# Final norm of a hybrid decoder step: the last token block in two pieces, and part of the outputs scaled on ScalarE and GpSimd

## The chip, the cores and the metric

The kernel runs on one core of a Trainium2 chip. The metric is the time of one execution on the device, in microseconds (us); lower is better. Times before are three runs, and one more execution was profiled.

## What is computed

The reference is one step of a decoder layer with retention heads, gated DeltaNet heads and a gated MLP, followed by a final norm. The part that matters here is its end, cut to a few lines:

```python
u, buf_ffn_new = causal_depthwise_conv(rms_norm(x, norm_ffn) @ w_up, buf_ffn, conv_ffn)
gate, val = jnp.split(u, 2, axis=-1)
x = x + (jax.nn.silu(gate) * val) @ w_down
...
def rms_norm(x, w):
    y = xf * lax.rsqrt(jnp.mean(xf * xf, axis=-1, keepdims=True) + EPS)
    return y * w
y_prompt = rms_norm(xp[:, N_META:], norm_final)
y_sample = rms_norm(xs, norm_final)
```

There are 1024 features (8 tiles of 128 partitions) and 1058 token columns: 32 sample tokens, 2 columns that are dropped, and 1024 prompt tokens.

## The kernel before

Features lie on the partitions and tokens in the columns. `ob` holds the residual stream, 8 feature tiles m by all columns. The MLP is worked through in 11 groups of two hidden tiles. In each group the up products, a convolution, the gate and the split of the product into a high and a low fp32r part (tiles `al` for the first token block, `as` for the others) come first. Then `down` (L1636) multiplies them with the down weights (`dhl`, `whi`, `wlo`), three matmuls for each of the two hidden tiles, six in all, into one of two PSUM banks of the ring "dn" (`mx3` and `mx4`), and VectorE adds the bank to `ob`, which frees it (L1646).

The token columns are cut by `BLK_B` (L47) into blocks of 510, 274 and 274. In the last group (`tail`), `final` (L1565) is called for each block in turn (L1664). It computes all eight `down` tiles of the block, squares `ob` on ScalarE, and adds the squares into two sums, the even m on GpSimd and the odd m on VectorE (L1576). Then TensorE sums over the partitions with a one-column matmul for each 128 columns (`pss`, L1582). VectorE copies these sums out of PSUM (L1589), scales them, ScalarE takes the root (L1593), VectorE the reciprocal and one step of refinement. A diagonal matrix `dg` for each 128 columns and a matmul with ones (L1603) spread the result over all partitions into the PSUM bank `rb`. VectorE multiplies each of the eight tiles by `nfin(m)` and `rb` in one instruction (L1607), and SP issues its transfer out (L1608).

What sets the order: every operation is recorded (`Recorder`, L209), and `flush` (L367) places all of them by a table of estimated costs and by priority classes, `with cls(n)`, a low number first. Class 0 here is the squares, sums and roots, class 1 the `down` products and additions, class 3 the outputs. So an output runs on VectorE where nothing more urgent is ready by that plan. Every engine then executes its own queue strictly in that order, and all instructions carry line 469 in the profile, where the plan is emitted. Buffers come from rings: "ds" for up to 276 columns, "f2k" for up to 512, and "c3" (names `c` in the profile) for the 128x4 numbers of the roots.

Of the kernel before, what the change touches and what calls it, by code (L numbers as in the profile page):

```python
# [17 lines left out]
AF = mybir.ActivationFunctionType  # L18
ALU = mybir.AluOpType
# [3 lines left out]
P = 128  # L23
D = 1024
# [11 lines left out]
EPS = 1e-6  # L36
# [10 lines left out]
BLK_B = ((0, 510), (510, 784), (784, 1058))  # L47
# [435 lines left out]
def build(tc, I, O, debug=None):  # L483
# [4 lines left out]
    V, S, G, T, DQ = (R.proxy(e) for e in "VSGTD")  # L488
# [11 lines left out]
    def buf(tag, shape, dt=None):  # L500
        v = R.tile(R.rings[tag])
        if dt is not None:
            v = v.bitcast(dt)
        n = 1
        for s in shape[1:]:
            n *= s
        v = v[0:shape[0], 0:n]
        if len(shape) == 3:
            v = v.rearrange("p (a b) -> p a b", a=shape[1])
        elif len(shape) == 4:  # L510
            v = v.rearrange("p (a b c) -> p a b c", a=shape[1], b=shape[2])
        return v
# [34 lines left out]
    def nfin(m):  # L547
        return wc[:, 69 + m:70 + m]
# [90 lines left out]
    with tc.tile_pool(name="mp", bufs=1) as mp:  # L639
# [54 lines left out]
        def x_stats(i, pss):  # L694
            b0, b1 = BLK_A[i]
            cs = slice(3 * i, 3 * i + 3)
            ms, mh, rs_, t_ = (b[:, cs] for b in (msx, mhx, rsx, tsx))
            for r, q0, q1 in ((MINI, 0, 1), (P, 1, 3)) if i == 0 else ((P, 0, 3),):
                V.tensor_scalar(out=ms[0:r, q0:q1], in0=pss[0:r, q0:q1], scalar1=1.0 / D, scalar2=EPS, op0=ALU.mult, op1=ALU.add)
            sqrt = S.activation(t_, ms, AF.Sqrt)  # L700
            V.tensor_scalar(out=mh, in0=ms, scalar1=-0.5, scalar2=None, op0=ALU.mult)
            V.reciprocal(rs_, t_)
            V.tensor_tensor(out=t_, in0=rs_, in1=mh, op=ALU.mult)
            V.tensor_tensor(out=t_, in0=t_, in1=rs_, op=ALU.mult)
            V.scalar_tensor_tensor(out=rs_, in0=t_, scalar=1.5, in1=rs_, op0=ALU.add, op1=ALU.mult)
            rb = bank()
            for c in range(3 * i, 3 * i + 3):
                c0, c1 = chunk_cols(c)
                r = c1 - c0
                dg = buf("jk", [r, r])  # L710
                V.tensor_scalar(out=dg, in0=ident[0:r, 0:r], scalar1=rsx[0:r, c:c + 1], scalar2=None, op0=ALU.mult)
                T.matmul(rb[:, c0 - b0:c1 - b0], ones_t[0:r, :], dg, start=True, stop=True)
            return rb, sqrt
# [21 lines left out]
        spread, _ = x_stats(0, sums)  # L735
# [537 lines left out]
    with tc.tile_pool(name="cp", bufs=1) as cp:  # L1273
# [20 lines left out]
        def f384():  # L1294
            return buf("f2k", [P, 512])
# [266 lines left out]

        uo0 = buf("uo", [P, 72])

        def final(t, wd):  # L1565
            c0, c1 = BLK_B[t]
            n = c1 - c0
            cuts = [(a, min(a + P, n)) for a in range(0, n, P)]
            acc = [tmp(n), tmp(n)]
            for m in range(KD):  # L1570
                down(wd[m // 2], m, t)
                with cls(0):
                    sq = tmp(n) if m > 1 else acc[m]
                    S.activation(sq[:, 0:n], ob[:, m, c0:c1], AF.Square)
                    if m > 1:
                        (V if m % 2 else G).tensor_tensor(out=acc[m % 2][:, 0:n], in0=acc[m % 2][:, 0:n], in1=sq[:, 0:n], op=ALU.add)  # L1576
            with cls(0):
                pss = bank()
                prev = None
                for i, (a, b) in enumerate(cuts):  # L1580
                    for j in range(2):
                        op = T.matmul(pss[0:b - a, i:i + 1], acc[j][:, a:b], ones_t[:, 0:1], start=j == 0, stop=j == 1)  # L1582
                        if prev is not None:
                            op.preds.add(prev)
                        prev = op
                s2, rr, tt, mm = (buf("c3", [P, 4]) for _ in range(4))
                G.memset(s2, 1.0)
                full = n // P
                V.tensor_copy(s2[:, 0:full], pss[:, 0:full])  # L1589
                if n % P:  # L1590
                    V.tensor_copy(s2[0:n % P, full:full + 1], pss[0:n % P, full:full + 1])
                V.tensor_scalar(out=mm, in0=s2, scalar1=1.0 / D, scalar2=EPS, op0=ALU.mult, op1=ALU.add)
                S.activation(tt, mm, AF.Sqrt)  # L1593
                V.tensor_scalar(out=mm, in0=mm, scalar1=-0.5, scalar2=None, op0=ALU.mult)
                V.reciprocal(rr, tt)
                V.tensor_tensor(out=tt, in0=rr, in1=mm, op=ALU.mult)
                V.tensor_tensor(out=tt, in0=tt, in1=rr, op=ALU.mult)
                V.scalar_tensor_tensor(out=rr, in0=tt, scalar=1.5, in1=rr, op0=ALU.add, op1=ALU.mult)
                rb = bank()
                dg = buf("f2k", [P, 4, P])  # L1600
                for i, (a, b) in enumerate(cuts):
                    V.tensor_scalar(out=dg[0:b - a, i, 0:b - a], in0=ident[0:b - a, 0:b - a], scalar1=rr[0:b - a, i:i + 1], scalar2=None, op0=ALU.mult)
                    T.matmul(rb[:, a:b], ones_t[0:b - a, :], dg[0:b - a, i, 0:b - a], start=True, stop=True)  # L1603
            with cls(3):
                for m in range(KD):
                    y = ob[:, m, c0:c1]
                    V.scalar_tensor_tensor(out=y, in0=y, scalar=nfin(m), in1=rb[:, 0:n], op0=ALU.mult, op1=ALU.mult)  # L1607
                    dma(out=O[0][m, :, c0:c1], in_=y)  # L1608

        for gp in range(NF // 2):  # L1610
            at = []
            uo = uo0 if gp == 0 else buf("uo", [P, 72])
            tail = gp == NF // 2 - 1

            def down_weights(mq, tags=("dhl", "dhl")):
                with cls(0):
                    raw = buf("rawd", [P, 2, 256])
                    dma(out=raw, in_=w_down[2 * gp * P:2 * gp * P + 2 * P, 256 * mq:256 * mq + 256].rearrange("(a p) m -> p a m", a=2))
                    dh, dl = (buf(t, [P, 2, 256]) for t in tags)
                    split(dh, dl, raw, G)  # L1620
                return dh, dl

            for p in (2 * gp, 2 * gp + 1):
                dg, dv = up_pair(p, uo, norm_first if p == 0 else None)
                row = []
                for t, (c0, c1) in enumerate(BLK_B):
                    n = c1 - c0
                    S.activation(dg[t][:, 0:n], dg[t][:, 0:n], AF.Silu)
                    G.tensor_tensor(out=dg[t][:, 0:n], in0=dg[t][:, 0:n], in1=dv[t][:, 0:n], op=ALU.mult)
                    ah, al = (buf("as" if t else "al", [P, n]) for _ in range(2))  # L1630
                    split(ah, al, dg[t][:, 0:n], V)
                    row.append((ah, al))
                at.append(row)
            dma(out=O[5][gp], in_=uo)

            def down(w, m, t):  # L1636
                c0, c1 = BLK_B[t]
                n = c1 - c0
                out = bank("dn")
                for i in range(2):  # L1640
                    dh, dl = (x[:, i, m % 2 * P:m % 2 * P + P] for x in w)
                    ah, al = at[i][t]
                    T.matmul(out[:, 0:n], dh, ah, start=i == 0, stop=False)
                    T.matmul(out[:, 0:n], dh, al, start=False, stop=False)
                    T.matmul(out[:, 0:n], dl, ah, start=False, stop=i == 1)
                V.tensor_tensor(out=ob[:, m, c0:c1], in0=out[:, 0:n], in1=ob[:, m, c0:c1], op=ALU.add)  # L1646

            R.stream = 1
            if not tail:

                wd = [down_weights(mq) for mq in range(2)]
                for m in range(4):
                    down(wd[m // 2], m, 0)
                for m in range(4):
                    for t in (1, 2):
                        down(wd[m // 2], m, t)
                for mq in (2, 3):
                    wd = down_weights(mq)
                    for m in (2 * mq, 2 * mq + 1):
                        for t in range(3):  # L1660
                            down(wd, m, t)
            else:
                wd = [down_weights(mq, ("dhl", "dhl") if mq < 2 else ("whi", "wlo")) for mq in range(4)]
                for t in range(3):  # L1664
                    final(t, wd)
            R.stream = 0
        R.flush()

# [60 lines left out]
```

## Time and profile before

| | |
|---|---|
| median of three runs | 1531.34 us (1531.19 to 1532.56) |
| the profiled execution, its own time | 1531.77 us |
| its span, first to last instruction | 1530.1 us (1530.06), mean granted clock 0.989 |
| TensorE matmuls busy | 1471.4 us, 96% |
| weight loads busy | 1329.2 us, 87% |
| VectorE (DVE) busy | 1127.7 us, 74% |
| ScalarE (ACT) busy | 643.9 us, 42% |
| GpSimd (POOL) busy | 459.6 us, 30% |

A row of the timeline gives the start in us from the span's start, the duration, the engine, the line, the operation, what it writes and reads by tile names, the shapes, how many instructions of that kind were merged (x2), and in brackets the idle time of the engine before it with what ended it. An instruction that stands and waits for a port inside its execution shows this as a longer duration. PE is TensorE, PEld its weight loads, SPq the queue that issues transfers.

### The profile page before, as it was taken

The numbers are of one execution on the slowest core, as the hardware profiler recorded it, in microseconds if no ns is written. First come the engines' busy times: TensorE is split into PE (matmuls) and PEld (weight loads), VectorE is DVE, ScalarE is ACT, GpSimd is POOL, SyncE is SP. The second block draws the span as 40 slices with busy tenths as digits, with TensorE's granted clock in tenths as the row PEclk, the third lists the DMA queues.
The fourth block names the chain that finished last, engine by engine and source line by source line (L and its number), as shares of the span: only waits on it lengthen the run. The fifth ranks groups of instructions, "written<-read, shape, count | busy, mean of one in ns | idle before, by whom it ended". The sixth has DMA issues, their size and how long they took to land.

```text
span 1530.1 us, 25981 instructions
## 1 busy us (share of the span) xinstructions
PE 1471.4 (96%) x9513; PEld 1329.2 (87%) x9513; DVE 1127.7 (74%) x2661; ACT 643.9 (42%) x1684; POOL 459.6 (30%) x502
## 2 busy tenths in 40 slices
PE   5999999999999999899899999999999999999996
PEld 4888988999889889898679989988998998899885
DVE  6877886787768856656887868677686867767677
ACT  4553464456345435433452434334242433424242
POOL 5321202302220221322643424333332433333341
PEclk9999999999999999999999999999999999999998
DMA  5120202112121201251111111121111111111103
GB/s 199 36 59 29 85 24 68 57 45 60 37 75 33 68 32 58 89 189 42 56 30 44 44 58 44 44 63 53 43 45 57 45 44 58 56 45 43 57 8 115
DMA packets 74653, 89.50 MB, mean 58 GB/s; under 512 B 19284, under 2 KB 49436, under 8 KB 74524
## 3 DMA queue, kind: packets, MB, share of 16 engines
q1 hardware_dynamic: 74524, 87.83, 18.1%
q8 instruction: 75, 1.23, 0.3%
q14 instruction: 54, 0.44, 0.1%
HBM read 78.14 MB, written 9.66 MB: 57 GB/s over the span
## 4 chain that ended last, share of the span: by engine, by line
PE 84%; DVE 11%; ACT 2%; issue 2%; DMA 1%; POOL 0%; SPq 0%; DVEq 0%; ACTq 0%; POOLq 0%
PE mx L469 45%; PE mm L469 39%; DVE ob L469 2%; DVE wlo L469 2%; DVE ds L469 1%; DVE c L469 1%; DVE hl L469 1%; DVE f2k L469 1%; DVE sw L469 1%; DVE t2k L469 0%; DVE wlox L469 0%; DMA ob<-in_xt 0%; DVE gvb L469 0%; ACT jk L469 0%; ACT hh L469 0%
## 5 line engine op out<-in xcount | busy, mean ns | idle before, releaser
L469 PE MATMUL mm<-hh,whi 128*128 128x384 f32 (+5 forms) x1084 | 357.7, 330 | 6.7 <-ACT hh L469 5.5
L469 PE MATMUL mm<-hl,whi 128*128 128x384 f32 (+5 forms) x1084 | 357.5, 330 | 2.9 <-DVE hl L469 2.9
L469 PE MATMUL mm<-hh,wlo 128*128 128x384 f32 (+5 forms) x1084 | 357.4, 330 | 0.0
L469 PEld LDWEIGHTS mm<-hh,whi 128*128 128x128 f32 x1084 | 206.6, 191 | 13.9 <-ACT hh L469 6.5
L469 PEld LDWEIGHTS mm<-hl,whi 128*128 128x128 f32 x1084 | 206.6, 191 | 9.9 <-DVE hl L469 4.2
L469 PEld LDWEIGHTS mm<-hh,wlo 128*128 128x128 f32 x1084 | 206.7, 191 | 4.3 <-issue 1.3
L469 DVE TENSOR_TENSOR ob<-mx,ob 128x274 f32<-128x274 f32 (+1 forms) x264 | 136.0, 522 | 99.5 <-PE mx L469 96.4
L469 PEld LDWEIGHTS mx<-as,dhl 128*128 128x128 f32 x1008 | 143.2, 190 | 16.7 <-DVE ob L469 8.5
L469 PE MATMUL mx<-as,dhl 128*128 128x274 f32 x1008 | 153.3, 293 | 1.4 <-DVE ob L469 0.4
L469 PE MATMUL mx<-al,dhl 128*128 128x510 f32 x504 | 134.2, 394 | 3.1 <-ACT al L469 2.0
L469 DVE TENSOR_TENSOR wlo<-raw,whi 128x512 fp32r<-128x512 f32 x125 | 118.0, 946 | 10.1 <-ACT whi L469 8.4
L469 ACT CAST whi<-raw 128x512 fp32r<-128x512 f32 x131 | 80.8, 618 | 101.6 <-PE mm L469 64.1
L469 DVE SCALAR_TENSOR_TENSOR f2k<-mx,wc,f2k 128x478 f32<-128x478 f32 x88 | 62.6, 712 | 62.4 <-ACT su L469 62.4
L469 PEld LDWEIGHTS mx<-al,dhl 128*128 128x128 f32 x504 | 89.3, 189 | 17.0 <-ACT al L469 2.3
L469 POOL TENSOR_TENSOR ob<-ob,sw 128x384 f32<-128x384 f32 (+1 forms) x39 | 40.9, 1049 | 178.5 <-DVE sw L469 136.1
L469 POOL TENSOR_TENSOR dhl<-rawd,dhl 128x512 fp32r<-128x512 f32 x42 | 54.5, 1298 | 132.9 <-ACT dhl L469 126.6
L469 PE MATMUL mx<-hl,whi 128*128 128x510 f32 x232 | 91.4, 394 | 0.0
L469 PE MATMUL mx<-hh,whi 128*128 128x510 f32 x232 | 91.0, 392 | 0.0
L469 PE MATMUL mx<-hh,wlo 128*128 128x510 f32 x232 | 90.8, 391 | 0.0
L469 POOL TENSOR_SCALAR f2k<-su,wc 128x32 f32<-128x32 f32 x44 | 13.9, 317 | 220.9 <-ACT su L469 220.9
L469 ACT ACTIVATE f2k<-mx,wc 128x478 f32<-128x478 f32 x44 | 29.1, 662 | 111.7 <-PE mx L469 111.6
L469 DVE SCALAR_TENSOR_TENSOR ds<-mm,wc,ds 128x274 f32<-128x274 f32 x132 | 63.0, 497 | 9.0 <-ACT ds L469 8.1
(377 smaller groups left out, 3513.3 us busy)
## 6 DMA issues: line engine op xcount, KB each, us to landing
raw<-in_w_in SPq DMA_DIRECT2D x64, 256.0 KB, 2.6
rawd<-in_w_down SPq DMA_DIRECT2D x44, 256.0 KB, 2.7
rawx<-in_w_up SPq DMA_DIRECT2D x44, 256.0 KB, 2.9
raw<-in_w_up SPq DMA_DIRECT2D x44, 256.0 KB, 2.6
gbq<-scr_rows SPq DMA_DIRECT2D x16, 256.0 KB, 4.2
out<-sst SPq DMA_DIRECT2D x8, 512.0 KB, 2.6
raw<-in_w_out SPq DMA_DIRECT2D x14, 256.0 KB, 2.8
ob<-in_xt SPq DMA_DIRECT2D x4, 768.0 KB, 8.7
```

Of the source, the lines that this page charges most:

```text
L469: f(*a, **k)
```

## The change

The final norm works on four pieces, listed in `FIN`, in place of three blocks: 510 and 274 columns as before, and the last block as 146 and 128 columns. `down` takes column bounds and slices the activations. In the first piece the odd squares too are added by GpSimd. The sums are scaled straight out of PSUM. The spread row `rb` is copied to SBUF (`rbs`) by ScalarE, and some of the outputs are made in two steps: ScalarE multiplies by `nfin(m)` in place, and GpSimd by `rbs`. The line that sets how many reads `i`, which the loops over `cuts` above it have assigned anew by then.

```diff
-        def final(t, wd):
-            c0, c1 = BLK_B[t]
+        FIN = ((0, 0, 510), (1, 510, 784), (2, 784, 930), (2, 930, 1058))
+        LAST = len(FIN) - 1
+
+        def final(i, wd):
+            t, c0, c1 = FIN[i]
             n = c1 - c0
             cuts = [(a, min(a + P, n)) for a in range(0, n, P)]
...
-                down(wd[m // 2], m, t)
+                down(wd[m // 2], m, t, c0, c1)
...
-                        (V if m % 2 else G).tensor_tensor(out=acc[m % 2][:, 0:n], in0=acc[m % 2][:, 0:n], in1=sq[:, 0:n], op=ALU.add)
+                        (V if m % 2 and i else G).tensor_tensor(out=acc[m % 2][:, 0:n], in0=acc[m % 2][:, 0:n], in1=sq[:, 0:n], op=ALU.add)
...
                 for i, (a, b) in enumerate(cuts):
...
-                s2, rr, tt, mm = (buf("c3", [P, 4]) for _ in range(4))
-                G.memset(s2, 1.0)
+                rr, tt, mm = (buf("c3", [P, 4]) for _ in range(3))
+                G.memset(mm, 1.0)
                 full = n // P
-                V.tensor_copy(s2[:, 0:full], pss[:, 0:full])
-                if n % P:
-                    V.tensor_copy(s2[0:n % P, full:full + 1], pss[0:n % P, full:full + 1])
-                V.tensor_scalar(out=mm, in0=s2, scalar1=1.0 / D, scalar2=EPS, op0=ALU.mult, op1=ALU.add)
+                for r, q0, q1 in ((P, 0, full), (n % P, full, full + 1)):
+                    if r and q1 > q0:
+                        V.tensor_scalar(out=mm[0:r, q0:q1], in0=pss[0:r, q0:q1], scalar1=1.0 / D, scalar2=EPS, op0=ALU.mult, op1=ALU.add)
...
             with cls(3):
+                aside = 4 if i == 0 else 3 if i == 1 else 2
+                rbs = f384()
+                S.copy(rbs[:, 0:n], rb[:, 0:n])
                 for m in range(KD):
                     y = ob[:, m, c0:c1]
-                    V.scalar_tensor_tensor(out=y, in0=y, scalar=nfin(m), in1=rb[:, 0:n], op0=ALU.mult, op1=ALU.mult)
+                    if m % 2 and m < 2 * aside:
+                        S.activation(y, y, AF.Copy, scale=nfin(m))
+                        G.tensor_tensor(out=y, in0=y, in1=rbs[:, 0:n], op=ALU.mult)
+                    else:
+                        V.scalar_tensor_tensor(out=y, in0=y, scalar=nfin(m), in1=rb[:, 0:n], op0=ALU.mult, op1=ALU.mult)
                     dma(out=O[0][m, :, c0:c1], in_=y)
...
-            def down(w, m, t):
-                c0, c1 = BLK_B[t]
+            def down(w, m, t, c0=None, c1=None):
+                a0 = BLK_B[t][0]
+                c0, c1 = (BLK_B[t] if c0 is None else (c0, c1))
...
-                    ah, al = at[i][t]
+                    ah, al = (x[:, c0 - a0:c1 - a0] for x in at[i][t])
...
-                for t in range(3):
-                    final(t, wd)
+                for i in range(len(FIN)):
+                    final(i, wd)
```

How the order moves is seen at three places. First TensorE at the very end, before the change: the last `down` product of the last block, the sums of squares (`mx_66`, from the two sums `ds`), and the spreading (`mx_68`).

```order
L469 MATMUL mx_69<-as_6482,whi_73 128x274
L469 MATMUL mx_69<-as_6481,wlo_77 128x274
L469 MATMUL mx_66<-ones_t,ds_6498 128x1
L469 MATMUL mx_66<-ones_t,ds_6499 128x1
...
L469 MATMUL mx_66<-ones_t,ds_6498 18x1
L469 MATMUL mx_66<-ones_t,ds_6499 18x1
L469 MATMUL mx_68<-f2k_6491,ones_t 128x128 x2
L469 MATMUL mx_68<-f2k_6491,ones_t 128x18
```

The same place after the change, from the spreading of the 146-column piece (`mx_68`) on; twelve `down` products of the 128-column piece follow it.

```order
L469 MATMUL mx_68<-f2k_6488,ones_t 128x128
L469 MATMUL mx_68<-f2k_6488,ones_t 128x18
L469 MATMUL mx_70<-as_6477,whi_73 128x128
L469 MATMUL mx_70<-as_6478,whi_73 128x128
L469 MATMUL mx_70<-as_6477,wlo_77 128x128
...
L469 MATMUL mx_69<-as_6481,wlo_77 128x128
L469 MATMUL mx_66<-ones_t,ds_6497 128x1
L469 MATMUL mx_66<-ones_t,ds_6493 128x1
L469 MATMUL mx_67<-f2k_6490,ones_t 128x128
```

Behind the last `down` product stand three matmuls in place of nine, and each `down` product of the last block is there twice, with fewer columns and the same weights.

Second, VectorE at the end, before the change, with the semaphores that an instruction waits for: the refinement of the root (`c`), the diagonals (`f2k`), and outputs (`ob<-ob,wc,mx`) of the second block (`mx_67`) and the third (`mx_68`).

```order
L469 SCALAR_TENSOR_TENSOR ob<-ob,wc,mx_67 128x274
L469 SCALAR_TENSOR_TENSOR c_6516<-c_6510,c_6516 128x4 [waits DVE_49]
L469 SCALAR_TENSOR_TENSOR ob<-ob,wc,mx_67 128x274
L469 TENSOR_SCALAR f2k_6491<-ident,c_6516 128x128 [waits DVE_49]
L469 TENSOR_SCALAR f2k_6491<-ident,c_6516 128x128
L469 TENSOR_SCALAR f2k_6491<-ident,c_6516 18x18
L469 SCALAR_TENSOR_TENSOR ob<-ob,wc,mx_67 128x274
L469 SCALAR_TENSOR_TENSOR ob<-ob,wc,mx_68 128x274 [waits PE_49]
L469 SCALAR_TENSOR_TENSOR ob<-ob,wc,mx_68 128x274 x7
```

The same place after it.

```order
L469 TENSOR_TENSOR c_6510<-c_6516,c_6515 128x4 [waits DVE_49]
L469 TENSOR_TENSOR c_6510<-c_6510,c_6516 128x4 [waits DVE_49]
L469 SCALAR_TENSOR_TENSOR c_6516<-c_6510,c_6516 128x4 [waits DVE_49]
L469 TENSOR_SCALAR f2k_6490<-ident,c_6516 128x128 [waits DVE_49]
L469 SCALAR_TENSOR_TENSOR ob<-ob,wc,mx_67 128x128 [waits Activation_49]
L469 SCALAR_TENSOR_TENSOR ob<-ob,wc,mx_67 128x128 x3
```

No output of an earlier piece stands between the steps of the last root any more, four outputs are left in place of eight, and the first of them waits for ScalarE in place of TensorE.

Third, GpSimd at the end after the change, where only sums of squares stood before: sums of the 128-column piece (`ds`), and the in-place products of the pieces of 146 and 128 columns (`ob`).

```order
L469 TENSOR_TENSOR ds_6497<-ds_6497,ds_6494 128x128
L469 TENSOR_TENSOR ob<-ob,f2k_6487 128x146 x3
L469 TENSOR_TENSOR ds_6497<-ds_6497,ds_6498 128x128
L469 TENSOR_TENSOR ob<-ob,f2k_6491 128x128 x4
```

The last sum of squares, on which the last root rests, stands behind three products of the piece before it.

## Rows read from the trace of the kernel before

**Rows 1.** The table of windows; columns by engine, instructions in brackets, granted clock, DMA

```profile
1505.00:1510.00 5.00, 4.94 (x42) 4.68 (x41) 4.54 (x15) 2.15 (x6) 0.81 (x2) 1.00 0.29 108
1510.00:1515.00 5.00, 3.63 (x26) 3.04 (x24) 4.80 (x15) 1.42 (x4) 1.53 (x2) 1.00 0.29 108
1515.00:1520.00 5.00, 1.82 (x12) 1.63 (x11) 4.50 (x16) 0.64 (x2) 0.00 (x0) 0.60 0.64 239
```

**Rows 2.** The chain of waits at the end: start us, us, what held it

```profile
1521.67 1.75 PE mx L469 x6
1523.42 0.02 issue
...
1524.36 2.46 DVE ob L469 x6
```

**Rows 3.** The timeline of TensorE, down products of the first and the last block

```profile
1488.70 0.64 PE L469 MATMUL mx<-al,whi 128*128 128x510 f32 x2
...
1489.41 0.63 PE L469 MATMUL mx<-al,whi 128*128 128x510 f32 x2
...
1503.09 1.03 PE L469 MATMUL mx<-as,dhl 128*128 128x274 f32 x6 [0.36 <-DVE ob L469]
...
1510.13 0.42 PE L469 MATMUL mx<-as,whi 128*128 128x274 f32 x2
...
1510.89 0.42 PE L469 MATMUL mx<-as,whi 128*128 128x274 f32 x2
```

**Rows 4.** The timeline of SP, and the list of transfers (size, us to landing)

```profile
1523.97 3.77 SPq L469 DMA_DIRECT2D out<-ob  x8
...
out<-ob SPq DMA_DIRECT2D x16, 137.0 KB, 1.9
```

**Rows 5.** The timeline of TensorE, sums of block 0 and spreading of block 1

```profile
1497.12 1.61 PE L469 MATMUL mx<-ones_t,f2k 128*128 128x1 f32 x14
1498.59 0.37 PE L469 MATMUL mx<-as,dhl 128*128 128x274 f32 x1
...
1513.02 0.93 PE L469 MATMUL mx<-f2k,ones_t 128*128 128x128 f32 x6
```

**Rows 6.** The timeline of GpSimd, two sums

```profile
1488.61 1.29 POOL L469 TENSOR_TENSOR f2k<-f2k,f2k 128x510 f32<-128x510 f32 x1 [1.94 <-ACT f2k L469]
...
1509.11 0.77 POOL L469 TENSOR_TENSOR ds<-ds,ds 128x274 f32<-128x274 f32 x1 [4.63 <-ACT ds L469]
```

**Rows 7.** The timeline of GpSimd and VectorE, where both work, and one undisturbed row

```profile
1501.45 0.79 POOL L469 TENSOR_TENSOR ds<-ds,ds 128x274 f32<-128x274 f32 x1 [2.33 <-ACT ds L469]
...
1501.57 0.69 DVE L469 TENSOR_TENSOR c<-c,c 128x4 f32<-128x4 f32 x1
...
1510.99 0.77 POOL L469 TENSOR_TENSOR ds<-ds,ds 128x274 f32<-128x274 f32 x1 [1.06 <-ACT ds L469]
...
1511.04 1.02 DVE L469 TENSOR_TENSOR ds<-ds,ds 128x274 f32<-128x274 f32 x1
...
1520.29 0.14 DVE L469 TENSOR_TENSOR c<-c,c 128x4 f32<-128x4 f32 x1
```

**Rows 8.** The timeline, sums of block 0, then the last block

```profile
1495.29 0.63 ACT L469 ACTIVATE f2k<-ob 128x510 f32<-128x510 f32 x1 [0.76 <-DVE ob L469]
...
1495.95 0.69 DVE L469 TENSOR_TENSOR f2k<-f2k,f2k 128x510 f32<-128x510 f32 x1 [0.25 <-ACT f2k L469]
...
1514.56 0.44 DVE L469 TENSOR_TENSOR ob<-mx,ob 128x274 f32<-128x274 f32 x1 [0.20 <-PE mx L469]
...
1515.04 0.43 ACT L469 ACTIVATE ds<-ob 128x274 f32<-128x274 f32 x1 [1.22 <-DVE ob L469]
1515.57 0.44 DVE L469 TENSOR_TENSOR ds<-ds,ds 128x274 f32<-128x274 f32 x1
1515.93 1.40 DVE L469 SCALAR_TENSOR_TENSOR ob<-ob,wc,mx 128x510 f32<-128x510 f32 x2
...
1516.07 1.66 PE L469 MATMUL mx<-ones_t,ds 128*128 128x1 f32 x10 [0.90 <-DVE ds L469]
```

## The prediction

> **What bounds the kernel now.** I read the page first: TensorE is busy 96% of the span (the table above), and everything until about 1490 us stays as it is, because the change touches only the last function. So I went to the end, with the table of windows [rows 1]: TensorE is full until 1510 us and almost empty from 1515, while VectorE is busy 4.5 to 4.8 of every 5 us until 1520; once TensorE has little to do its granted clock falls towards 0.5, the lower of its two levels. The chain of waits [rows 2] and the instructions of the last block in order [rows 3, 8] show the three stretches of the end. (a) The down products of the last block run from 1503.09 [rows 3] to about 1514.5, between VectorE's additions that free their banks. (b) From there the chain is the last addition, square, mean (1516.07, [rows 8]), roots on VectorE with scaled outputs of earlier blocks in between, spread matmuls from 1521.67, done at 1523.42 [rows 2]: 8.9 us. (c) From 1523.44 eight scaled outputs, their transfers and the landing, to 1530.1. SP issues eight transfers in 3.77 us, 1523.97 to 1527.74 [rows 4]; a step costs it about 0.48 although VectorE delivers an output every 0.41 [rows 2].
>
> **The sum.** It is made on the profiled execution, whose span ends at 1530.06; its own time is 1531.77, 0.4 above the median of the runs. I add the difference to the median 1531.34.
>
> *(a) Two pieces in place of one.* A down product of 274 columns costs TensorE 0.127 us: six lie between 1510.13 and 1510.89 [rows 3]. The change makes 96 of them, of 146 and 128 columns, from 48. No row shows such a product at under 274 columns, so I bound it. From below: 510 columns take 0.235 (three in 0.71, [rows 3]), so a column is worth 0.00046, and 146 and 128 columns come to 0.068 and 0.060. From above: a product of full f32 data at 128 columns is two records of 0.11 [rows 5], 0.22 us. I take 0.11: fourteen one-column matmuls against a 128-column, 4-byte weight take 1.47 us, 0.105 each and 0.11 with what lies around it [rows 5], so loading such a weight already needs that, and every down product loads a new one. TensorE's own time in the stretch was 48 x 0.127 = 6.1, plus spreading block 0 (8 records, 0.9), the sums of block 1 (1.0) and its spreading (0.9, [rows 5]): 8.9 of 11.4 us, so 2.5 idle. Now it is 96 x 0.11 = 10.6, the same 2.8, and new here the sums (0.55) and spreading (0.5) of the 146-column piece: 14.4. I keep the 2.5 idle, as VectorE still does other work between the additions.
>
> GpSimd comes in here. Two of its in-place products are 510 wide, 1.29 each [rows 6]. While GpSimd works on SBUF, a VectorE instruction whose operands are all in SBUF stands still: a product of 128x4, 0.14 alone, took 0.69 and ended with GpSimd's sum, and a 274-column sum of 0.44 took 1.02 [rows 7]. The Trainium skill, SBUF — State Buffer, section "SBUF: two separate sides", has it as an exclusive lock on a shared port pair, on which the loser fully blocks; these rows agree, and the rule speaks against this change. Additions queued behind such a stop free their bank late. One filled bank of six matmuls (0.66) covers part of each stop: at most 2 x (1.29 - 0.66) = 1.3 shows, at least 0; I take 0.7. The last down product then ends at 1503.1 + 14.4 + 2.5 + 0.7 = 1520.7, where it was 1514.5.
>
> *(b) The chain behind it* now covers 128 columns, and few outputs of earlier blocks are left to stand in between. A step starts 0.04 to 0.1 after what it waits for [rows 8]. In steps, start included: addition 0.34 (0.44 and 0.69 at 274 and 510 columns, [rows 8], give 0.28 at 128), square 0.36, sum 0.37, four records for the mean 0.65, the mean read from PSUM by the scaling itself 0.21, root 0.25, half and reciprocal 0.31, three dependent products 0.17 each, diagonal 0.29, one spread product 0.56 with its start: 3.85 in place of 8.9. Against it: GpSimd's sum of squares m=6 stands behind three 146-column products of 0.49 (from 0.77 and 1.29, [rows 6]); I charge 0.4 of them, between 0 (hidden behind the last matmuls) and 1.5. Spreading ends at 1520.7 + 4.25 = 1524.95, where it was 1523.42.
>
> *(c) The end.* The order shows that VectorE's first output of each block waits for ScalarE's copy of the spread row, no longer for TensorE: 0.06 + 0.31 + 0.09 more, for a copy of 128 columns (0.43 at 274, 0.63 at 510, [rows 8], give 0.31). An output takes 0.33, so SP starts at 1525.75 in place of 1523.97. It still has eight transfers: 3.77 again. GpSimd's four products (4 x 0.45 = 1.8) and VectorE's four (1.05) both fit under that, so dividing the outputs buys nothing here. The kernel's end lay 2.32 behind the last issue (1527.74 to 1530.06); I keep this, though the transfers are half as large. Sum: 1525.75 + 3.77 + 2.32 = 1531.85 against 1530.06, **+1.8 us**.
>
> *Edits at nothing.* Block 0's odd squares move to GpSimd, whose last 510-column sum ends 0.6 later than VectorE's did (1496.64, [rows 8]). This is hidden because the root's result waited about 1 us behind additions on VectorE anyway; without that, 0.6. ScalarE gains eleven scalings and four copies of 0.3 to 0.7; it was busy 0.6 to 2.2 of 5 us [rows 1]. A square behind such a copy would delay a sum by 0.6 at most. The removed copies of the sums save about 0.1 per block, counted in (b). Transfers grow from 24 to 32; each waits for the landing of the eighth before it, 1.9 us [rows 4], under 8 x 0.48. The number of outputs put aside is not what its line says: the inner loops over cuts reuse the name i, so it is 2, 2, 3 and 4 for the four pieces. By (c) the four at the end still fit under SP; at least nothing, at most 0.4 if the last GpSimd product came last.
>
> So I forecast 1531.34 + 1.8 = **1533.1 us**, inside the 0.2% (3.06 us, 1528.28 to 1534.40) that a measurement can tell from no change. Its own range is 1531.5 to 1535.
>
> **The rivals.** *Short products pay four passes* (slower, 0.15). If a product under some width runs like full f32, 0.22 to 0.25, the 96 cost 12 us more, of which at most the 3.2 idle is absorbed: +8.8, 1542. For it: no row shows a short one. Against: only its weight load is known to be long.
>
> *The port* (slower, 0.18). GpSimd's first seven products sum to 2 x 1.29 + 2 x 0.77 + 3 x 0.49 = 5.6 us, of which I charged 1.1. If each finds VectorE at an instruction with SBUF operands and additions behind it, 4.5 more lands on the path: 1537.6. It turns slower than 0.2% once 1.3 more does. For it: both long cases of [rows 7]. Against: outputs and additions, the larger part of VectorE's work, read PSUM, and ran undisturbed beside GpSimd.
>
> *Weight loads hide* (no change, 0.12). Products at 0.064 take 4.4 off TensorE, but VectorE's own work in (a) is about 15.8 us (six 510-column outputs at 0.66, from two in 1.40 [rows 8], six of 274 at 0.41, sixteen short additions at 0.21, sums, roots), so only 2.0 is won: 1531.1. The Trainium skill, TensorE: Matmul & The Clock Gate, section "Back-to-back issue gap", gives 81 ns for sustained 128-column products; by it 96 x 0.03 = 2.8 would go, again capped at 2.0. No run here shows it.
>
> *VectorE alone sets the end* (faster, 0.10). It is the busiest engine from 1510 [rows 1]. Two 510-column and ten 274-column outputs become nine short ones of 0.27 (-3.0), one 510-column sum goes (-0.6), sixteen short additions in place of eight cost 0.5: -3.1, 1528.2. Against it: the matmuls and SP's issues don't shrink.
>
> **How the numbers follow.** The forecast has 0.45. Of it 0.34 lies within 0.2% and 0.11 above. With the four-pass rival (0.15) and most of the port (0.16), slower has 0.42; the last rival gives 0.06 to faster and the hidden loads 0.02: 0.08; the rest, 0.50, is no change. The range leaves out the four-pass case and half of the last rival, and reaches to the port's 1537.6: 1529 to 1538.
>
> **What would show it.** Steps of 0.11 between down products of 146 and 128 columns; the last of them ending near 1520.7; VectorE instructions of 128x4 that last until a GpSimd product ends; an idle gap on VectorE in front of the last outputs that ends with ScalarE's copy; eight last transfers still taking 3.8 us. Steps of 0.2 or an end of the down products before 1518 would prove the sum wrong.

## The result, and the profile after

The changed kernel takes 1541.83 us (median of six runs, 1540.92 to 1543.68) against 1531.26 for the kernel before: a ratio of 1.0066, 95% interval 1.0056 to 1.0076. That is 10.6 us between the medians, 10.1 by the ratio, and clear of noise. One of the six runs behind the 1531.26 took 4960.27 us; without it that median is 1531.19. The forecast was 1533.1 with a range of 1529 to 1538, so the time lies outside it.

| | before | after |
|---|---|---|
| the profiled execution, its own time | 1531.77 us | 1540.92 us |
| its span | 1530.1 us | 1539.2 us |
| mean granted clock | 0.989 | 0.983 |
| TensorE matmuls busy | 1471.4 us | 1483.5 us |
| weight loads busy | 1329.2 us | 1340.7 us |
| VectorE busy | 1127.7 us | 1126.2 us |
| ScalarE busy | 643.9 us | 652.1 us |
| GpSimd busy | 459.6 us | 470.1 us |

The engines that were given work have a little more of it, and VectorE hardly less. The result shows in the 12 us more that TensorE is busy. Where they lie is seen in the table of windows of the changed kernel (columns as in [rows 1]: the stretch, then the busy us of TensorE's matmuls, its weight loads, VectorE, ScalarE and GpSimd, each with its instructions in brackets, then the granted clock, the DMA share and GB/s):

```profile
1505.00:1510.00 5.00, 4.09 (x32) 3.87 (x31) 4.27 (x15) 2.52 (x7) 3.04 (x4) 0.81 0.42 157
1510.00:1515.00 5.00, 5.00 (x24) 4.73 (x23) 2.34 (x9) 1.50 (x5) 1.79 (x3) 0.50 0.44 161
1515.00:1520.00 5.00, 5.00 (x28) 4.97 (x27) 3.27 (x10) 1.74 (x6) 0.53 (x2) 0.50 0.45 167
1520.00:1525.00 5.00, 5.00 (x24) 4.82 (x23) 2.86 (x16) 1.38 (x5) 0.91 (x2) 0.50 0.31 108
1525.00:1530.00 5.00, 4.45 (x19) 4.09 (x18) 3.05 (x11) 1.86 (x6) 1.85 (x4) 0.50 0.29 92
```

Before, the clock was 1.00 until 1515 and 0.60 in the mean from 1515 to 1520 [rows 1]: 1.0 us of it at full and the rest at half, so it fell at 1516.0, behind the last of the down products. Now the mean from 1505 to 1510 is 0.81, so it fell at 1508.1, and from there TensorE works at half clock, 1.2 GHz, with hardly a pause for 20 us. The timeline of TensorE shows what that does to one product:

```profile
1502.07 0.83 PE L469 MATMUL mx<-as,dhl 128*128 128x146 f32 x6
...
1508.67 0.70 PE L469 MATMUL mx<-as,whi 128*128 128x146 f32 x2 [0.91 <-DVE ob L469]
1509.17 0.41 PE L469 MATMUL mx<-as,wlo 128*128 128x146 f32 x1
1509.39 0.63 PE L469 MATMUL mx<-as,whi 128*128 128x146 f32 x2
1509.81 0.41 PE L469 MATMUL mx<-as,wlo 128*128 128x146 f32 x1
...
1519.21 2.82 PE L469 MATMUL mx<-as,dhl 128*128 128x128 f32 x12
1521.83 0.63 PE L469 MATMUL mx<-as,whi 128*128 128x128 f32 x2
...
1528.00 0.41 PE L469 MATMUL mx<-as,wlo 128*128 128x128 f32 x1
...
1531.90 0.80 PE L469 MATMUL mx<-f2k,ones_t 128*128 128x128 f32 x2 [1.76 <-DVE f2k L469]
```

The six of 146 columns at 1502.07 take 0.83 us with the tail of the last: 0.11 each. From 1509.17 to 1509.81 three start, 0.21 each, and the twelve of 128 columns from 1519.21 to 1521.83 take 2.62: 0.21 to 0.22 each. The last down product ends at 1528.4 and the last spreading at 1532.70. The chain of waits says the same in one line, 84 TensorE instructions with nothing in between:

```profile
1508.67 18.47 PE mx L469 x84
...
1527.17 0.30 DVE ob L469
```

From the spreading on the end goes much as forecast. In the timeline of the other engines (and, last, of SP) the copy of the spread row starts at 1532.73, VectorE's first output waits for it, GpSimd's products run beside VectorE's, and SP's eight issues take 3.65 us. The first three rows are for the point on the port below, and the fourth, GpSimd's last sum of squares, is for the point on (b).

```profile
1505.73 0.75 DVE L469 SCALAR_TENSOR_TENSOR ob<-ob,wc,mx 128x510 f32<-128x510 f32 x1 [0.98 <-ACT f2k L469]
...
1507.05 1.27 POOL L469 TENSOR_TENSOR ob<-ob,f2k 128x510 f32<-128x510 f32 x1
...
1507.39 0.95 DVE L469 TENSOR_SCALAR c<-c 128x4 f32<-128x4 f32 x1
...
1527.95 0.45 POOL L469 TENSOR_TENSOR ds<-ds,ds 128x128 f32<-128x128 f32 x1 [0.49 <-ACT ds L469]
...
1532.73 0.27 ACT L469 COPY f2k<-mx 128x128 f32<-128x128 f32 x1 [2.08 <-PE mx L469]
1533.03 1.12 DVE L469 SCALAR_TENSOR_TENSOR ob<-ob,wc,mx 128x128 f32<-128x128 f32 x4 [1.19 <-ACT f2k L469]
1533.07 1.52 POOL L469 TENSOR_TENSOR ob<-ob,f2k 128x128 f32<-128x128 f32 x4 [4.67 <-ACT f2k L469]
...
1533.40 3.65 SPq L469 DMA_DIRECT2D out<-ob  x8
```

### The profile page after: what moved, and what is told of

Read it like the earlier page. It is cut to its first block, busy times and chain, and to the rows that moved or that the text cites. A ratio compares the mean times of both kernels' runs of the same rounds, so it can differ in the third digit from the quotient of the medians.

```text
span 1539.2 us, 26146 instructions
## 1 busy us (share of the span) xinstructions
PE 1483.5 (96%) x9561; PEld 1340.7 (87%) x9561; DVE 1126.2 (73%) x2669; ACT 652.1 (42%) x1708; POOL 470.1 (31%) x520
## 4 chain that ended last, share of the span: by engine, by line
PE 84%; DVE 10%; issue 2%; ACT 1%; DMA 1%; POOL 1%; SPq 0%; POOLq 0%; ACTq 0%; DVEq 0%
PE mx L469 46%; PE mm L469 39%; DVE ob L469 2%; DVE wlo L469 2%; DVE ds L469 1%; DVE c L469 1%; DVE f2k L469 1%; DVE hl L469 1%; DVE sw L469 1%; DVE t2k L469 1%; DVE wlox L469 0%; DVE gvb L469 0%; DMA ob<-in_xt 0%; ACT jk L469 0%; DMA m<-scr_rows 0%
## 5 line engine op out<-in xcount | busy, mean ns | idle before, releaser
L469 DVE TENSOR_TENSOR ob<-mx,ob 128x274 f32<-128x274 f32 (+3 forms) x272 | 137.4, 511 | 109.0 <-PE mx L469 105.9
L469 PEld LDWEIGHTS mx<-as,dhl 128*128 128x128 f32 x1032 | 148.2, 193 | 16.5 <-DVE ob L469 8.3
L469 PE MATMUL mx<-as,dhl 128*128 128x274 f32 (+2 forms) x1032 | 158.1, 295 | 1.2 <-DVE ob L469 0.2
```

The costliest lines, as they stand in the source:

```text
L469: f(*a, **k)
```

## The experiments

Theory 1: the split products let TensorE's granted clock fall 8 us too early, and everything after is paid at half clock. Theory 2: the clock fell because the outputs on ScalarE and GpSimd hold VectorE up and TensorE waits, or for another reason in that stretch; then the short products are not the cause.

The profiled spans differ by up to a few us before the change even begins, so the table has a second measure beside the ratio: the **stretch** from the first down product of the last block to the end of the span, both read from the same profile (before: 1503.09 [rows 3] to 1530.06, 27.0). "Clock falls" is worked out from the mean clock of the window in which it falls, as above.

| kernel | median us | ratio to before (95%) | clock falls | stretch us |
|---|---|---|---|---|
| the change | 1541.83 | 1.0066 (1.0056 to 1.0076) | 1508.1 | 37.1 |
| x1_three: all but the split | 1532.34 | 1.0003 (0.9994 to 1.0011) | 1518.8 | 27.0 |
| x2_split: the split alone | 1539.27 | 1.0055 (1.0036 to 1.0074) | 1508.8 | 37.2 |
| x3_wide: the change, wide products | 1533.85 | 1.0012 (1.0001 to 1.0022) | 1527.3 | 30.2 |
| x4_wide_v: the split, wide, outputs on VectorE | 1534.90 | 1.0021 (1.0012 to 1.0030) | 1529.6 | 29.7 |
| x7_half_wide: only the 146-column piece wide | 1534.84 | 1.0017 (1.0009 to 1.0026) | 1521.6 | 32.1 |
| y4_filler: the change and 16 wide products more | 1535.11 | 1.0021 (1.0012 to 1.0030) | 1526.1 | 30.8 |
| y1_counts_split: the change, counts 4, 3, 2, 2 | 1539.67 | 1.0057 (1.0045 to 1.0069) | 1507.2 | 37.2 |
| x5_counts: three pieces, counts 4, 3, 2 | 1532.11 | 0.9993 (0.9985 to 1.0002) | 1518.1 | 26.8 |
| x6_pairs: x5, last block in four transfers | 1532.69 | 1.0001 (0.9992 to 1.0010) | 1520.3 | 27.2 |
| y2_two_queues: x5, half the last issues on ScalarE | 1530.35 | 0.9992 (0.9983 to 1.0001) | 1516.8 | 26.6 |
| y3_fill_end: y2 and 19 products more | 1532.16 | 1.0003 (0.9994 to 1.0012) | 1520.8 | 27.3 |

The last two columns come from one profiled execution of each kernel, but the mean granted clock over the whole span is on record for every run. Falls ahead of the last block are in it too. It is 0.981 to 0.984 in the six runs of the change, 0.988 to 0.991 in the twelve of x3_wide and 0.989 to 0.991 in the ten of y4_filler; the change does not overlap with the other two, so what their profiles show is no chance of one execution. Within x2_split the shortest of the six runs, 1535.83 us, has 0.987 and the longest, 1545.69, has 0.979. The profile of x7_half_wide is the longest of its twelve runs (1539.12 us at 0.985, where seven others have 0.990), so its stretch is not that of the median.

### Which part of the change costs it

**x1_three**

```diff
-        FIN = ((0, 0, 510), (1, 510, 784), (2, 784, 930), (2, 930, 1058))
+        FIN = ((0, 0, 510), (1, 510, 784), (2, 784, 1058))
```

> All of the change except the split: the last block stays one piece of 274 columns, so every down product has 274 or 510 columns. Theory 1 (the split products, of 146 and 128 columns, made the granted clock of TensorE fall at 1508.1 instead of 1516.0 us, and every later product then took 0.21 instead of 0.11): no short products, so the clock falls at 1514 us or later and the time is 1529 to 1533 us. Theory 2 (the outputs that ScalarE and GpSimd make hold VectorE up, its late additions let TensorE idle, and the idle time brought the clock down): they are still there, so the clock falls near 1508 again and the time is 1536 us or more.

Measured: 1532.34, no difference from before, stretch 27.0. The table of windows:

```profile
1505.00:1510.00 5.00, 3.96 (x34) 3.64 (x32) 4.36 (x12) 1.97 (x5) 2.94 (x4) 1.00 0.42 155
1510.00:1515.00 5.00, 3.68 (x26) 3.14 (x24) 4.45 (x14) 2.44 (x6) 2.85 (x5) 1.00 0.44 162
1515.00:1520.00 5.00, 1.40 (x12) 1.21 (x12) 4.85 (x18) 0.64 (x2) 0.42 (x1) 0.88 0.74 265
```

Here TensorE is busy only 3.96 and 3.68 of 5 us, waiting for VectorE's additions, and the clock stays at full until 1518.8. Theory 2 falls as far as the outputs go: the moved outputs are there, they do make TensorE wait (it was busy 4.94 of 5 us from 1505 to 1510 before, [rows 1]), and the clock holds all the same.

**x2_split**: the kernel before with `FIN`, the loop over it and `down` with column bounds; outputs, odd squares and sums as they were.

> The split alone in the kernel before: all outputs on VectorE, odd squares of the first block on VectorE, sums copied out of PSUM as before. Theory 1: the granted clock falls at 1507 to 1511 us, the down products of the last pieces then start 0.21 apart, and the time is 1538 to 1543 us. Theory 2: nothing runs on GpSimd but sums of squares, so the clock holds until about 1520 and the time is 1531 to 1535 us.

Measured: 1539.27, stretch 37.2, the same as the whole change. The table of windows:

```profile
1505.00:1510.00 5.00, 4.73 (x39) 4.54 (x38) 4.54 (x17) 1.51 (x5) 0.53 (x2) 0.88 0.42 160
1510.00:1515.00 5.00, 5.00 (x24) 4.73 (x23) 3.22 (x12) 1.30 (x4) 1.04 (x3) 0.50 0.35 128
```

TensorE is busy 4.73 of 5 us, more than in x1_three, and yet the clock falls at 1508.8. So the split alone makes the loss, and the busy share of a window does not tell whether the clock will hold.

### Is it the clock, or are short products slow?

**x3_wide**: the same 96 products and weight loads, each over all 274 columns of the block.

```diff
-                n = c1 - c0
+                n = BLK_B[t][1] - a0
...
-                    ah, al = (x[:, c0 - a0:c1 - a0] for x in at[i][t])
+                    ah, al = (x[:, 0:n] for x in at[i][t])
...
-                V.tensor_tensor(out=ob[:, m, c0:c1], in0=out[:, 0:n], in1=ob[:, m, c0:c1], op=ALU.add)
+                V.tensor_tensor(out=ob[:, m, c0:c1], in0=out[:, c0 - a0:c1 - a0], in1=ob[:, m, c0:c1], op=ALU.add)
```

> The whole change, but each down product of the two last pieces multiplies all 274 columns of the block, and the half that the piece does not need is left in PSUM: the same 96 products and weight loads with twice the columns, so more work for TensorE. Theory 1: the granted clock stays at full until the last down products, about 1520 us; they start 0.127 apart and end near 1521, and the time is 1532 to 1536 us, some 8 us less than the change although TensorE does more. Theory 2: the clock falls near 1508 as with the change; a product of 274 columns then takes at least 0.228 and the time is 1542 to 1545 us.

Measured: 1533.85, stretch 30.2. Twice the columns through TensorE make the kernel 6.9 us shorter in the stretch than the change:

```profile
1510.00:1515.00 5.00, 4.08 (x28) 3.61 (x28) 4.59 (x17) 2.21 (x7) 2.32 (x5) 1.00 0.71 264
1515.00:1520.00 5.00, 4.61 (x39) 4.35 (x38) 4.73 (x19) 2.30 (x8) 1.07 (x3) 1.00 0.67 238
1520.00:1525.00 5.00, 4.17 (x31) 3.71 (x29) 4.80 (x20) 2.69 (x9) 2.75 (x6) 1.00 0.48 157
```

The clock is 1.00 in all three windows. VectorE, at 4.6 to 4.8 of 5 us, is now the busiest engine. One thing stays mixed here: the products are wider and the clock is higher. The next two take that apart.

**x7_half_wide**: the change, with `w0, w1 = (0, 274) if c0 == 784 else (c0 - a0, c1 - a0)` as the columns of a product, so that the short ones begin only with the 128-column piece.

> The whole change, with only the products of the 146-column piece widened to 274 columns; the 128-column piece keeps its short products. Theory 1 (short products bring the clock down): no short ones run until about 1517 us, so the clock holds past 1517, at most the later part of 48 products runs at half clock, and the time lies between the wide kernel (1533.9) and the change (1541.8): 1534 to 1538 us. Theory 2 (something else in the stretch from 1500 to 1508, the sums, the spreading or the waits, brings it down): the clock falls near 1508 to 1510 and the time is 1541 us or more.

Measured: 1534.84, stretch 32.1. The timeline of TensorE in the 128-column piece:

```profile
1518.87 1.94 PE L469 MATMUL mx<-as,dhl 128*128 128x128 f32 x14
1520.67 0.44 PE L469 MATMUL mx<-as,whi 128*128 128x128 f32 x2
1520.94 0.28 PE L469 MATMUL mx<-as,wlo 128*128 128x128 f32 x1
1521.06 0.38 PE L469 MATMUL mx<-as,whi 128*128 128x128 f32 x2
1521.28 0.28 PE L469 MATMUL mx<-as,wlo 128*128 128x128 f32 x1
...
1521.97 0.63 PE L469 MATMUL mx<-as,whi 128*128 128x128 f32 x2
1522.40 0.41 PE L469 MATMUL mx<-as,wlo 128*128 128x128 f32 x1
```

Three products of 128 columns start from 1520.94 to 1521.28, 0.11 each, and two from 1521.97 to 1522.40, 0.215 each. The clock fell at 1521.6, between the two. The same short product takes about half as long on one side of that moment as on the other. The sums and the spreading of the earlier blocks are as in the change, and up to 1521.6 the clock holds through them, so they do not bring it down by themselves.

**y4_filler**: the short products as in the change, and one unread product of 510 columns behind each six.

```diff
-                    T.matmul(out[:, 0:n], dl, ah, start=False, stop=i == 1)
+                    last = T.matmul(out[:, 0:n], dl, ah, start=False, stop=i == 1)
+                if c0 > a0 or c1 < BLK_B[t][1]:
+                    fb = bank("mm")
+                    fill = T.matmul(fb[:, 0:510], wd[3][0][:, 1, P:2 * P], at[1][0][0], start=True, stop=True)
+                    fill.preds.add(last)
```

> The whole change with its 96 short products as they are, and behind each six of them one product of 510 columns whose result nobody reads: 16 more products, so more work for TensorE and nothing less. Theory 1 (the short products themselves cost 0.11, and the falling clock doubles it): the clock holds past 1515 us, the short products keep 0.11, 16 extra ones cost 16 x 0.22 = 3.5 us of which the idle time takes a part, and the time is 1533 to 1537 us, less than the change. Theory 2 (the clock falls for another reason, or the short products are slow by themselves): 16 more products at 0.43 on top of the change, 1544 to 1549 us.

Measured: 1535.11, stretch 30.8. First the timeline of TensorE, then two of its windows:

```profile
1516.96 0.78 PE L469 MATMUL mx<-as,dhl 128*128 128x128 f32 x6
1517.58 0.45 PE L469 MATMUL mm<-al,whi 128*128 128x510 f32 x1
1517.86 0.78 PE L469 MATMUL mx<-as,dhl 128*128 128x128 f32 x6
```

```profile
1510.00:1515.00 5.00, 5.00 (x37) 4.30 (x37) 4.93 (x18) 2.73 (x8) 2.32 (x5) 1.00 0.66 245
1515.00:1520.00 5.00, 5.00 (x42) 4.68 (x41) 4.65 (x22) 2.27 (x8) 0.79 (x3) 1.00 0.81 280
```

Six products of 128 columns start between 1516.96 and 1517.58, between two of the fillers: 0.103 each in the mean, and 0.11 from the third on, which starts at 1517.13. The short product is not slow; with 16 products more, and nothing less, the kernel is 6.3 us shorter in the stretch than the change. It is 3.8 longer than before the change, about what the 16 fillers take (3.5 by the expectation). That the early fall of the clock causes the loss is shown, from both sides: it falls early with the short products alone, and does not in the kernel with wider ones or in this one, with wide ones among the short. Why the short products bring it down is not shown.

### The other parts of the change

**x4_wide_v**: x2_split with the wide products of x3_wide.

> The split with products widened to 274 columns, so that the clock holds, and nothing else of the change: all outputs on VectorE, odd squares of the first piece on VectorE, sums copied out of PSUM. Against the wide kernel with the whole change (span 1534.4 us, VectorE busy 4.6 to 4.8 of 5 us from 1510 to 1525) it tells what the moved outputs are worth at full clock. Theory R (they relieve VectorE, which is what ends last there): eleven outputs come back to VectorE, two of 510, two of 274, three of 146 and four of 128 columns, some 4.5 us of its time, of which 2 to 4 lie on the path: 1536 to 1538 us. Theory P (GpSimd's products hold VectorE up through the port, the copy of the spread row and GpSimd's queue add a wait, as the prediction charged with 1.6 us): 1531.5 to 1533 us. In both the clock holds until after 1520.

Measured: 1534.90, stretch 29.7. It lies between the two theories. By the ratios the moved outputs are worth 1.0021 - 1.0012, 1.4 us, but the intervals overlap; by the stretches (29.7 and 30.2, 37.2 and 37.1, 27.0 and 27.0 without and with them) they are worth nothing. Neither theory is borne out as it was put; the runs look as if relief and waits about cancel, which was not tested further.

**y1_counts_split**: `aside` set at the top of `final`, ahead of the loops that reuse `i`.

> The whole change, with the number of outputs set aside as its line says (4, 3, 2 and 2 for the four pieces, where the reused name made it 2, 2, 3 and 4). Theory 1 (the end is set by short products at half clock; VectorE was busy only 2.3 to 3.3 of 5 us from 1510 to 1530): the name changes nothing that ends last, the clock falls before 1511 us again, 1540 to 1543 us. Rival: the four products on GpSimd at the very end (1.5 us) matter after all, then 1 to 2 us less than the change.

Measured: 1539.67, a third of a us under the band, ratio 1.0057. The clock falls at 1507.2 and the stretch is 37.2, as in the change, so what the median is lower by is not seen in this part, and the intervals of the two ratios overlap. No cost of the name is seen here. **x5_counts** makes the same edit with three pieces.

> Three pieces as before the change, and the outputs set aside as the line on aside says (4, 3 and 2 for the three blocks, where the reused name made it 2, 2 and 2). Three more outputs leave VectorE, two of 510 and one of 274 columns, 1.7 us. Theory R (VectorE ends last until 1520): 0.8 to 1.7 us less than the three-piece kernel with 2, 2, 2, so 1530 to 1531.5. Theory P (each product on GpSimd costs VectorE as much by the port): no less, or up to 1.3 us more. The clock falls at 1516 or later.

Measured: 0.9993 against 1.0003 for x1_three, stretch 26.8 against 27.0: at most a tenth of a percent, with overlapping intervals. The median, 1532.11, is above the band of theory R, and the stretch gives 0.2 us of its 0.8 to 1.7. Whether it is a gain stays open.

### SP's issues, and a faster version

**x6_pairs**: in the last block, one transfer for each two tiles.

> The kernel with counts 4, 3 and 2 and three pieces; the last block leaves in four transfers of two tiles in place of eight of one. The prediction held that SP's eight issues, 0.48 us apart, set the end behind the last spreading. If so, four steps go: 1.0 to 1.9 us less than with eight. If the outputs themselves or the landing set the end, at most 0.4 less, or a little more because a pair waits for its second tile.

Measured: no gain, 1.0001, stretch 27.2 where x5_counts has 0.9993 and 26.8. Four steps of SP less do not bring the end forward. The list of transfers has the four with 3.2 us to landing, where single tiles took 1.9 before [rows 4]:

```profile
out<-ob SPq DMA_DIRECT2D x4, 274.0 KB, 3.2
```

**y2_two_queues**

```diff
-                    dma(out=O[0][m, :, c0:c1], in_=y)
+                    (S if t == 2 and m % 2 else DQ).dma_start(out=O[0][m, :, c0:c1], in_=y)
```

> Three pieces with counts 4, 3 and 2; of the last block's eight transfers the four odd ones are issued by ScalarE in place of SP, each still one tile. If the eight steps of SP (0.48 us each) set the end behind the outputs (VectorE's six end 2.55 us after its first): 1.0 to 1.5 us less than the same kernel with SP alone (median 1532.1, span 1528.1). If the landing or the outputs set it: within 0.4 of it.

Measured: 0.9992 against 0.9993 for x5_counts, stretch 26.6 against 26.8, so within 0.4. Two windows at the end of x5_counts, then two of this one (the last two columns are the share of the DMA engines and GB/s):

```profile
1524.00:1525.00 1.00, 0.00 (x0) 0.00 (x0) 0.00 (x0) 0.00 (x0) 0.00 (x0) 0.50 0.85 283
1525.00:1526.00 1.00, 0.00 (x0) 0.00 (x0) 0.00 (x0) 0.00 (x0) 0.00 (x0) 0.50 0.83 282
```

```profile
1522.00:1523.00 1.00, 0.00 (x0) 0.00 (x0) 0.78 (x2) 0.00 (x0) 0.00 (x0) 0.50 1.04 349
1523.00:1524.00 1.00, 0.00 (x0) 0.00 (x0) 0.00 (x0) 0.00 (x0) 0.00 (x0) 0.50 1.02 340
```

With one queue the DMA engines are 0.83 to 0.85 busy, with two they are full, and the rate goes from 283 to 340 GB/s. A transfer of 137 KB takes 0.41 us at that rate, an estimate from this window, and SP's step is 0.48. So at this size SP's step and the moving of the data cost nearly the same, and taking the one away leaves the other. This kernel has the lowest ratio of those tried, 0.08% below before with an interval that reaches 1.0001: better than the change, not shown to be better than before or than x5_counts.

**y3_fill_end**: y2 with 7 products behind the last down product and 12 behind the last sum.

> The kernel with two queues, and 19 products of 274 columns whose results nobody reads, 7 behind the last down product and 12 behind the last sum, where TensorE stood idle. Theory 1 (what TensorE multiplies decides the granted clock): the clock holds until the last spreading, the six spreading records take 0.93 in place of 1.75 us, and the time is 0.5 to 1.0 us less than without them. Rival: the clock falls as before, near 1518, and the extra products, 0.23 each, push the spreading back: 0.5 to 2 us more.

Measured: 1.0003 against 0.9992 for y2_two_queues, stretch 27.3 against 26.6, so 0.7 to 1.7 us more, as the rival has it. The clock fell at 1520.8, soon after the twelve had begun. The last block also began later in this execution, at 1504.24 in place of 1500.23; counted from there the clock fell after 16.5 us in both kernels.

```profile
1516.90 1.06 PE L469 MATMUL mm<-as,whi 128*128 128x274 f32 x7
...
1520.10 2.58 PE L469 MATMUL mm<-as,whi 128*128 128x274 f32 x12
...
1522.48 1.59 PE L469 MATMUL mx<-f2k,ones_t 128*128 128x128 f32 x6
```

Seven took 1.06 us, twelve, most of them at half clock, 2.58, and the spreading began 0.78 us behind the first diagonal (1521.70), where it was 0.34 in y2_two_queues. In y4_filler extra products held the clock while TensorE had other work throughout; put into a stretch that is mostly idle they did not, and stood in the way. That is one execution: five of the eleven runs have a mean clock of 0.990 to 0.992, where the profiled one has 0.988, and whether it held longer in them is open.

## Why the prediction was wrong

**The step that failed** is the price in part (a), "now it is 96 x 0.11 = 10.6", where all 96 were charged at full clock. The first 24 ran at it; the other 72 ran at 0.21, behind the fall of the granted clock at 1508.1. The prediction had read the clock [rows 1], but only as something that falls once TensorE has little to do. It never asked what the clock would do while TensorE was full of shorter products, and none of its rivals did. Steps of 0.2, which it named as a sign of a wrong sum, are what the trace shows.

- The sizes by the forecast's own sum: 24 x 0.11 + 72 x 0.213 = 18.0, 7.4 more than 10.6. The sums and the spreading, also mostly at half clock, come to 5.95 in place of 3.85 (six spreading records take 1.69 at 1511.31 where they took 0.93, [rows 5]). Part (a) lasted from 1502.07 to 1528.4, 26.3 us, where 17.6 were forecast; the rest of it, 2.4, is idle time, where 3.2 were charged for idle time and port. 7.4 and 2.1 more, 0.8 less: that is the 8.7 by which (a) is longer. It began 1.0 earlier, so its end is 7.7 late, and so is all behind it.
- **The product at full clock** was right: 0.11 taken, 0.103 to 0.11 measured. The weight loads are as far apart (in the change five from 1503.13 take 0.63 us, 0.11 each and the tail of the last), as argued from [rows 5]. Halving the columns brought the product only from 0.127 to 0.11.
- **(b)** came out right in its total, in part by luck: from the last down product to the end of the spreading 4.3 us, forecast 4.25. GpSimd's sum did not wait behind the three products, for which 0.4 was charged: GpSimd stood idle for 0.49 in front of it. But the last spreading took 0.80 at half clock, with its start 0.85, where 0.56 was put down, and VectorE's last sum of squares started 0.13 after its square was done, behind outputs of the piece before.
- **(c)** was right. First issue 0.7 later, eight issues 3.65, landing and end 2.15 (1537.05 to 1539.2): forecast 0.8, 3.77 and 2.32. VectorE's first output does wait for ScalarE's copy.
- **Without the fall of the clock** the sum would have come near: the wide kernel, whose products cost 0.127 as [rows 3] have it, measures 1.0012, 1.8 us over before (0.2 to 3.4 by the interval), and the forecast was +1.8. By the stretch it is 3.2 longer than before. The agreement of 1.8 with 1.8 is partly luck, since 96 wide products cost 1.6 us more than short ones at full clock.
- **The port** (0.7 charged): one case shows, the row of 128x4 at 1507.39 that lasts 0.95 and ends with GpSimd's product at 1508.3, and TensorE idles 0.91 in front of 1508.67. The charge was of the right size; the rival that put 4.5 us there was wrong. VectorE also stood for 0.98 in front of 1505.73, until ScalarE had copied the first block's spread row; the prediction charged that wait only at the end.
- **Four passes** gave 1542, and the time is 1541.83. The number came out by a mechanism that is not there: the same products run at 0.103 to 0.11 in y4_filler. Its price of 0.22 and the half clock's 0.21 are alike by chance. A forecast that only checked the time would have called this rival confirmed.
- **Weight loads hide** fell: no six short products in a row ran under 0.10 each in any run. The Trainium skill, TensorE: Matmul & The Clock Gate, section "Back-to-back issue gap", gives 81 ns for 128 columns; these runs, with 4-byte weights, do not reach it.
- **VectorE alone sets the end** fell too: in x3_wide VectorE is the busiest engine, and the kernel is still not faster than before.
- **Edits at nothing**: the odd squares on GpSimd, the means from PSUM and the reused name all lie within what x1_three and y1_counts_split leave: nothing that these runs can tell from zero.

## What to carry to other kernels

Before a change shortens the products of an engine whose clock is granted, ask what the clock will do, and price every product at both levels: here the same product costs 0.11 or 0.21, and a range that leaves out the second price cannot hold the time. A busy share near 100% does not say that the clock will hold. And a rival whose number fits is not yet confirmed: look for its step in the rows, or change the one thing it rests on.

## What the runs showed of the hardware that was not expected

- The granted clock fell from 2.4 to 1.2 GHz while TensorE was busy 4.73 of 5 us with products of 146 columns and one-column sums (x2_split), and stayed at 2.4 while it was busy 3.68 of 5 with products of 274 (x1_three). The Trainium skill, TensorE: Matmul & The Clock Gate, section "HAM oscillation — how this bites in real kernels", names gaps in which TensorE stands idle as what brings the clock down; the trace differs, for in x2_split the longest gap between 1502 us and the fall was 0.35 us, and the kernel with the longer gaps (1.04 us in front of 1509.13 in x1_three) kept it.
- Once it had fallen, 15 us of short products, sums and spreading without a pause (the change, 1510 to 1525 at 5.00 of 5) did not bring it back; in y3_fill_end, after the twelve products of 274 columns, it was up again from 1524.2 to 1527.6, too late to be of use.
- A short product's step, 0.103 to 0.11 us at 2.4 GHz, is 0.21 at 1.2 GHz. The weight load follows the clock too: one of 128 columns lasts 0.19 us at the higher level (before, 1514.11) and 0.33 at the lower (the change, 1527.25).
- The eight last transfers of 137 KB move at 283 GB/s from one queue and at 340 from two, with the DMA engines full. In the change, of 64 KB each, they move at 130 to 133 GB/s with the DMA engines 0.44 to 0.45 busy (1534 to 1538 us), while SP's eight issues take 3.65 us.
